# Delta output projection by Strassen products with tokens on partitions, weight sums moved to the heads

## The chip, the core and the metric

One NeuronCore of a Trainium2 chip runs the kernel. It has a matrix engine (PE, with its weight loads shown as PEld), a vector engine (DVE), a scalar engine (ACT), GpSimd (POOL) and a sync engine (SP) on whose queue this kernel puts all its transfers; 16 DMA engines carry them. The metric is the device time in microseconds (us) of one execution. Three timed runs of the kernel before gave 2934.2, 2929.16 and 2933.91: the median is 2933.91.

## What is computed

A hybrid decoder layer for 512 tokens and a model width of 2048, in float32: sliding-window attention and a gated DeltaNet run side by side on the same normalised input, their outputs are merged by gates and projected.

```python
h = rms_norm(x, norm_w) * (1.0 + scale) + shift
proj = h @ w_in                      # q, k, v, gate of attention; q, k, v, z, b, a of delta; merge gates
...
y_a = a_out @ w_o_swa                # 2048 -> 2048
...
o = gated_delta_rule(dq, dk, dv, g, beta)
o = rms_norm(o, dn_norm_w) * jax.nn.silu(dz)
y_b = o.reshape(B, T, DN_VAL).astype(x.dtype) @ w_o_dn      # 4096 -> 2048
y = jax.nn.sigmoid(mg_a) * y_a + jax.nn.sigmoid(mg_b) * y_b
return x + gate * (y @ w_out)        # 2048 -> 2048
```

The change is about `y_b`, the delta projection: 32 heads of 128 channels, 4096 in all, times a 4096 x 2048 matrix.

## The kernel before

**Products.** Each float32 factor is split into a high and a low part (`split`: ACT copies to the matrix type, DVE subtracts), and each product of 128x128 by 128x512 is three matmuls (`mm3`: lines 240, 241 and 242 in the kernel before): high x high, high x low, low x high. A *tile* is 128 output channels by 512 tokens (`channel_tile`): 16 steps of three matmuls, 48 in all, with the weights as the stationary factor and the tokens streaming, so that the result has channels on partitions.

**Weights.** `jobs` is a list of weight blocks of 1 MB in the order of use. `load_job` loads one into one of two `raw` buffers; `split_half` makes high and low parts of half a block (`whi`, `wlo`, 128x1024 each) in one of three buffers; `half_done` queues the next of both. The output stage takes three of five raw blocks from a further buffer (`rawo`).

**Order.** The program is written as generators. Every six matmuls `pump` takes a step of what is under way: `go` for work that belongs to the current tiles, `paced` for slow work at so many units per pump, `beside` for work at so many steps per pump. A scheduler then fixes each engine's own order; an engine does not go past an instruction that waits. `behind` ties an instruction to a place after the last matmul. All transfers stand in SP's order, and each of them also waits for the transfer that was issued eight places earlier.

**Stages.** Startup to about 180 us (conditioning, norm, first tiles); the keys; attention; the delta heads, 16 groups from about 1150 to 2187, of which each makes five tiles, loads two rows of decay masks (`E`, made on POOL and ACT), and writes two head outputs of 256 KB each to `o_d`; the delta projection (`branch_b`) from 2188.3 to 2595.2; the attention projection (16 tiles `os`) to 2769; the output projection by one step of Strassen's algorithm. For the last, `PRODUCTS` (line 34) lists seven products instead of eight: each with its name, the combination ("form") of the four quarters of the tokens' matrix that it takes, and either a quarter of the weights or one of four sums of quarters (`weight_sums`).

**The delta projection before.** `branch_b` works in two halves of 2048 channels. For each half it loads 16 blocks of `o_d`, splits them into `oh` and `ol`, computes two tiles of the merge gate (`ma` 12 and 13, then 14 and 15, by `merge_gate`), and then 16 tiles `od`. The first half is stored to `yb_d` with channels on partitions; the second adds it and multiplies with 1 + the merge gate from `mb_d`. Beside it run the output gate (`gate`: 16 loads of 1 MB, a sum on DVE, four matmuls) and `weight_sums` for the output projection (per set four loads of 512 KB, four additions of 128x1024 on DVE and four stores; eight sets).

## Time and profile before

| what | value |
|---|---|
| median of three timed runs | 2933.91 us |
| profiled execution | 2929.78 us, span 2928.0 us |
| instructions in the span | 38184 |
| DMA over the span | 498.34 MB, mean 170 GB/s |
| granted PE clock, mean | 0.995 |

Busy time by stage (us from the span's start; times in us, clock as a share of full speed):

| stage | length | PE | DVE | ACT | DMA share | GB/s |
|---|---|---|---|---|---|---|
| keys (180 to 600) | 420.0 | 420.0 | 277.4 | 197.1 | 0.53 | 166 |
| heads (1150 to 2187) | 1037.0 | 1029.4 | 554.7 | 403.5 | 0.38 | 119 |
| delta projection (2188.3 to 2595.2) | 406.9 | 399.8 | 213.6 | 112.5 | 0.84 | 293 |
| attention projection (2595.2 to 2769) | 173.8 | 173.8 | 88.0 | 53.7 | 0.59 | 192 |
| output projection (2769 to 2928) | 159.0 | 152.7 | 105.3 | 62.9 | 0.72 | 258 |

A stage in which PE's busy time equals its length is set by PE; where it falls short, PE waited for something. Matmuls overlap in the pipeline, so the cost of one is the distance between starts and not its duration. Idle time of an engine that nobody waits for costs nothing. The DMA share is the mean busy share of the 16 DMA engines.

### The profile page before, as it was taken

How to read it: one execution, taken by the hardware profiler on the slowest of the kernel's cores; microseconds unless marked ns; L12 is line 12 of the kernel's file. 1: busy time of each engine (PE TensorE's matmuls, PEld its weight loads, DVE VectorE, ACT ScalarE, POOL GpSimd, SP SyncE). 2: the span in 40 equal slices, each digit the busy share in tenths (PEclk: the TensorE clock that was granted, in tenths of full speed). 3: DMA queues.
4: the chain of work that ended last, by engine and by line, in shares of the span. 5: the costliest groups of instructions: out<-in, count | busy, mean ns of one | idle time of the engine just before them, and what ended most of it. 6: DMA issues, size and time to landing. Idle time of an engine off the chain costs nothing.

```text
span 2928.0 us, 38184 instructions
## 1 busy us (share of the span) xinstructions
PE 2861.4 (98%) x14524; PEld 2346.6 (80%) x14524; DVE 1755.9 (60%) x2903; ACT 1128.6 (39%) x2295; POOL 130.9 (4%) x124
## 2 busy tenths in 40 slices
PE   6899999999999999999999999999999999999999
PEld 5578888877877878888888888888887887888887
DVE  5756666868768666666544445455445555434666
ACT  3356443234444333333533334344333232222443
POOL 0001000100001010000000000001000000000000
PEclk8999999999999999999999999999999999999999
DMA  9856654322253243333533333343338988855794
GB/s 329 320 172 194 202 164 143 120 78 91 96 139 104 84 162 110 122 111 114 158 116 124 109 122 115 117 135 115 109 127 306 315 319 294 288 171 176 243 321 172
DMA packets 184874, 498.34 MB, mean 170 GB/s; under 512 B 75217, under 2 KB 77777, under 8 KB 147313
## 3 DMA queue, kind: packets, MB, share of 16 engines
q1 hardware_dynamic: 184690, 495.90, 51.1%
q8 instruction: 114, 1.87, 0.3%
q14 instruction: 70, 0.57, 0.1%
HBM read 415.26 MB, written 78.33 MB: 169 GB/s over the span
## 4 chain that ended last, share of the span: by engine, by line
PE 86%; DMA 5%; DVE 5%; ACT 2%; issue 1%; SPq 0%; POOL 0%; DVEq 0%; POOLq 0%; ACTq 0%
PE mm L240 23%; PE mm L242 23%; PE mm L241 23%; DMA oraw<-o_d 2%; PE m L241 2%; PE m L242 2%; PE m L240 2%; DMA gw<-in_w_ada_gate 1%; DVE wa L410 1%; PE pv L894 1%; PE po L913 1%; PE O L1259 1%; PE S L1208 1%; PE pP L281 1%; ACT sm L1232 1%
## 5 line engine op out<-in xcount | busy, mean ns | idle before, releaser
L240 PE MATMUL mm<-hh,whi 128*128 128x512 f32 x2784 | 1132.1, 407 | 2.8 <-ACT mth L270 2.8
L242 PE MATMUL mm<-hh,wlo 128*128 128x512 f32 x2784 | 1089.9, 391 | 1.1 <-DVE wlo L62 1.1
L241 PE MATMUL mm<-hl,whi 128*128 128x512 f32 x2784 | 1086.9, 390 | 0.0
L62 DVE TENSOR_TENSOR wlo<-raw,whi 128x1024 fp32r<-128x1024 f32 (+1 forms) x484 | 597.5, 1235 | 485.8 <-ACT whi L61 470.0
L61 ACT CAST whi<-raw 128x1024 fp32r<-128x1024 f32 (+1 forms) x484 | 504.7, 1044 | 914.7 <-PE mm L241 811.6
L242 PEld LDWEIGHTS mm<-hh,wlo 128*128 128x128 f32 x2784 | 522.8, 188 | 115.7 <-DVE wlo L62 1.6
L240 PEld LDWEIGHTS mm<-hh,whi 128*128 128x128 f32 x2784 | 523.9, 188 | 111.7 <-issue 8.3
L241 PEld LDWEIGHTS mm<-hl,whi 128*128 128x128 f32 x2784 | 524.5, 188 | 98.5 <-issue 0.5
L240 PE MATMUL mm<-oh,whi 128*128 128x512 f32 x512 | 201.7, 395 | 5.4 <-ACT oh L61 5.4
L241 PE MATMUL mm<-ol,whi 128*128 128x512 f32 x512 | 200.2, 391 | 0.5 <-DVE ol L62 0.5
L242 PE MATMUL mm<-oh,wlo 128*128 128x512 f32 x512 | 200.1, 391 | 0.1
L240 PEld LDWEIGHTS mm<-oh,whi 128*128 128x128 f32 x512 | 96.5, 188 | 27.7 <-ACT oh L61 7.1
L709 ACT ACTIVATE E<-E,neg_g 128x128 f32<-128x128 f32 x256 | 82.3, 394 | 86.0 <-POOL E L703 86.0
L241 PEld LDWEIGHTS mm<-ol,whi 128*128 128x128 f32 x512 | 96.6, 189 | 22.8 <-DVE ol L62 1.8
L242 PEld LDWEIGHTS mm<-oh,wlo 128*128 128x128 f32 x512 | 96.5, 188 | 20.6 <-DVE wlo L62 0.5
L738 DVE TENSOR_TENSOR atmp<-A 128x62 f32<-128x62 f32 (+30 forms) x124 | 109.4, 882 | 0.6
L746 DVE TENSOR_TENSOR A<-A,atmp 128x62 f32<-128x62 f32 (+30 forms) x124 | 107.9, 870 | 0.6
L841 POOL TENSOR_TENSOR qe<-qe,yq 128x512 f32<-128x512 f32 x32 | 52.8, 1669 | 955.8 <-DMA qe<-eg_rows 696.8
L887 DVE SCALAR_TENSOR_TENSOR r<-pp,neg_eg,vt 128x128 f32<-128x128 f32 x96 | 29.2, 346 | 86.3 <-PE pp L884 84.8
L1232 ACT ACTIVATE sm<-sm,mx,rs 128x256 f32<-128x256 f32 (+1 forms) x128 | 71.7, 562 | 3.5 <-DVE mx L1227 3.5
L573 DVE SCALAR_TENSOR_TENSOR yv<-mm,convh,yv 128x511 f32<-128x511 f32 (+2 forms) x96 | 71.3, 743 | 1.4
L703 POOL TENSOR_SCALAR_AFFINE_SELECT E<-E 128x512 f32<-128x512 f32 x64 | 48.2, 767 | 436.4 <-DMA E<-g_rows 366.1
(335 smaller groups left out, 2952.5 us busy)
## 6 DMA issues: line engine op xcount, KB each, us to landing
raw<-in_w_ch SPq DMA_DIRECT2D x158, 1024.0 KB
wa<-in_w_ada_ss SPq DMA_DIRECT2D x32, 1024.0 KB
raw<-in_w_od SPq DMA_DIRECT2D x32, 1024.0 KB
E<-g_rows SPq DMA_DIRECT2D x64, 256.0 KB
q<-in_w_out SPq DMA_DIRECT2D x32, 512.0 KB
gw<-in_w_ada_gate SPq DMA_DIRECT2D x16, 1024.0 KB
f_d<-q SPq DMA_DIRECT2D x32, 512.0 KB
raw<-in_w_os SPq DMA_DIRECT2D x16, 1024.0 KB
```

The lines of the kernel that those rows point to most:

```text
L61: self.nc.scalar.copy(out=hi, in_=src)
L62: self.nc.vector.tensor_tensor(out=lo, in0=src, in1=hi.bitcast(F32), op=ALU.subtract)
L240: nc.tensor.matmul(ps, lhsT=wh, rhs=xh, start=first, stop=False)
L241: nc.tensor.matmul(ps, lhsT=wh, rhs=xl, start=False, stop=False)
L242: self.last_mm = nc.tensor.matmul(ps, lhsT=wl, rhs=xh, start=False, stop=last)
L573: nc.vector.scalar_tensor_tensor(out=y[:, s:], in0=ps[:, : T - s], scalar=w[:, j : j + 1], in1=y[:, s:], op0=ALU.mult, op1=ALU.add)
L703: self.last_mask = self.nc.gpsimd.affine_select(out=E, in_=E, pattern=[[0, NTB], [1, P]], compare_op=ALU.is_ge, fill=NEG, base=0, channel_ ...
L709: self.nc.scalar.activation(E[:, c, :], E[:, c, :], AF.Exp, bias=self.neg_g[:, c, h : h + 1])
L738: eng.tensor_tensor(out=t, in0=A[:, m : m + 1, m + 1 :].to_broadcast([P, m, n]), in1=A[:, :m, m : m + 1].to_broadcast([P, m, n]), op=ALU.mult,
L746: self.behind(eng.tensor_tensor(out=A[:, :m, m + 1 :], in0=A[:, :m, m + 1 :], in1=t, op=ALU.add))
L841: self.behind(nc.gpsimd.tensor_tensor(out=qf, in0=qf, in1=q, op=ALU.mult), masks)
L1232: nc.scalar.activation(t, t, AF.Exp, scale=r[:, h : h + 1], bias=mx[:, h : h + 1], accum_out=den[:, h : h + 1])
```

## The change

The delta projection takes the form of the output projection. `w_od` is laid out in quarters ("quads"). Each half of channels h and each half n of the output columns is computed by the seven products of `PRODUCTS`, in the order m1, m7, m5, m2, m6, m4, m3: 28 products of 48 matmuls instead of 32 tiles of 48. The *tokens* are now the stationary factor and the weights stream, so results have tokens on partitions. `delta_forms` makes the seven forms of a half from `o_d`: for h = 0 five go to slots `f0` to `f4` and two through one staging buffer (`late`) to DRAM (`b_d`), to be loaded into `x0` and `x1` once the normalised input is no longer needed; for h = 1 two go to `x2` and `x3` and five through staging, to be loaded into `x`/`f` slots as these come free during (h, n) = (0, 1). `delta_evict` combines products into output blocks; h = 0 stores them to `yo_d`; h = 1 adds the stored ones, transposes each block on PE (16 groups of four) and multiplies with 1 + the merge gate. All four merge tiles now stand before the projection. Quarter sums of `w_od` (two sets of eight) join those of `w_out`, and all three run in the heads from group 4. The gate moves to the keys. One out of three weight blocks of the projection goes to a third raw buffer (`braw`).

```diff
-        for half in range(2):
-            ma(range(12 + 2 * half, 14 + 2 * half))
-            jobs += [(f"od{half}_{j}", a["w_od"][half, j]) for j in range(KT)]
+        ma(range(12, 16))
+        self.od0 = len(jobs)
+        for half in range(2):
+            for n in range(2):
+                for m, (_, _, q, f) in enumerate(PRODUCTS):
+                    for i in range(2):
+                        src = a["w_od"][half, 2 * q[0] + n, 2 * q[1] + i] if q else self.g_d[half, n, f, i]
+                        jobs.append((f"od{half}{n}_{m}_{i}", src))
+        self.od1 = len(jobs)
...
+            if self.od0 <= j < self.od1:
+                own = (j - self.od0) % 3 < 2
...
+            self.beside(self.gate(gt), 0.18, "gate")
...
+                if g == 4:
+                    sums = self.paced(self.weight_sums(ws), 1.55)
...
+            self.drain_slow(sums)
...
     def branch_b(self):
...
-            for half in range(2):
-                for kt in range(KT):
-                    raw = wk.tile([P, T], F32, tag="oraw", name="oraw")
-                    nc.sync.dma_start(out=raw, in_=self.o_d[half * KT + kt])
-                    self.split(oh[:, kt, :], ol[:, kt, :], raw)
-                for j in range(2):
-                    self.merge_gate("ma", 12 + 2 * half + j, self.ma_d)
...
+            self.go(self.delta_forms(wk, w, 0, A[0], 0), 1)
+            for j in range(12, 16):
+                self.merge_gate("ma", j, self.ma_d)
+            self.drain_live()
...
+            A[0].update(zip(forms[5:], more))
+            for f in forms[5:]:
+                self.form_load(0, f, A[0][f])
+            A[1].update(zip(forms, more[2:]))
+            build = self.paced(self.delta_forms(wk, w, 1, A[1], 1), 1.0)
...
+            for h, n, m in items:
+                name, form = PRODUCTS[m][:2]
+                if (h, n, m) == (0, 1, 1):
+                    self.drain_slow(build)
+                if h == 0 and n == 1 and 1 <= m <= 5:
+                    A[1][forms[m + 1]] = slots[m - 1]
+                    self.form_load(1, forms[m + 1], slots[m - 1])
...
+                ah, al = A[h][form]
+                for p in range(4):
+                    hi, lo = self.half(f"od{h}{n}_{m}_{p // 2}")
+                    for t in range(2):
+                        for k in range(2):
+                            kt, cols, tsl = 2 * p + k, slice(k * T, k * T + T), slice(t * P, (t + 1) * P)
+                            self.mm3(ps[name, t], (ah[:, kt, tsl], al[:, kt, tsl]), (hi[:, cols], lo[:, cols]), kt == 0, kt == 7)
...
+    def delta_forms(self, wk, w, h, direct, pause):
...
+        def put(kt, f, src):
+            if f in direct:
+                self.split(direct[f][0][:, kt, :], direct[f][1][:, kt, :], src)
+                return
+            k = staged.index(f) % 2
+            if k == 0:
+                late[0] = wk.tile([P, 2, 2, 256], F32R, tag="late", name="late", bufs=1)
+            t = late[0]
+            self.split(t[:, k, 0, :], t[:, k, 1, :], src)
+            for x in range(2):
+                nc.sync.dma_start(out=self.b_d[h, order[f], x][:, kt, :], in_=t[:, k, x, :].bitcast(F32))
...
+    def form_load(self, h, f, slot):
+        k = [p[1] for p in PRODUCTS].index(f)
+        for x in range(2):
+            self.nc.sync.dma_start(out=slot[x].bitcast(F32), in_=self.b_d[h, k, x])
...
+    def delta_evict(self, w, pf, h, n, name, ps, keep):
...
+            nc.sync.dma_start(out=prev, in_=self.yo_d[cc, t])
...
+            yield 2
+            TT(out=src, in0=src, in1=prev, op=ALU.add)
+            yield 1
+            pt = pf.tile([P, 4, P], F32, tag="tp", name="pty", bufs=2)
+            self.transpose4(pt.rearrange("p j t -> p (j t)"), lambda j: src[:, j * P : (j + 1) * P])
+            STT(out=th, in0=th, scalar=1.0, in1=pt, op0=ALU.add, op1=ALU.mult)
```

What stands where, on the engines that the change reorders. DVE before, after the last heads and at the first `od` tiles (`wlo` is the low part of a weight half, `ol` that of the heads' outputs, `gate_bc` the gate's sum):

```order
L62 TENSOR_TENSOR wlo_18601<-raw_18477,whi_18600 128x1024
L62 TENSOR_TENSOR ol_18387<-oraw_18412,oh_18386 128x512
L62 TENSOR_TENSOR ol_18387<-oraw_18416,oh_18386 128x512
L62 TENSOR_TENSOR wlo_18633<-raw_18541,whi_18632 128x1024
L62 TENSOR_TENSOR ol_18387<-oraw_18420,oh_18386 128x512
L62 TENSOR_TENSOR ol_18387<-oraw_18424,oh_18386 128x512
L1435 SCALAR_TENSOR_TENSOR gate_bc_18501<-gw_18581,silu_c_118,gate_bc_18501 128x2048
L62 TENSOR_TENSOR ol_18387<-oraw_18428,oh_18386 128x512
L62 TENSOR_TENSOR ol_18387<-oraw_18432,oh_18386 128x512
L62 TENSOR_TENSOR wlo_18667<-raw_18541,whi_18666 128x1024
```

DVE in the changed kernel at merge tile 14, whose two halves are `wlo_19178` and `wlo_19209` (`f0l` to `f4l` are forms, `o0` and `o1` the heads' outputs, `late` the staging buffer):

```order
L62 TENSOR_TENSOR wlo_19178<-raw_18875,whi_19177 128x1024
L62 TENSOR_TENSOR f0l_18838<-o0_18865,f0h_18837 128x256
L62 TENSOR_TENSOR f1l_18840<-s3_18877,f1h_18839 128x256
L1074 TENSOR_TENSOR o0_18865<-o0_18865,o1_18866 128x256
L62 TENSOR_TENSOR f3l_18844<-o1_18866,f3h_18843 128x256
...
L62 TENSOR_TENSOR f4l_18846<-o0_19075,f4h_18845 128x256
L1074 TENSOR_TENSOR o0_19109<-o0_19109,o1_19110 128x256
L62 TENSOR_TENSOR wlo_19209<-raw_18875,whi_19208 128x1024
```

Between two weight halves stood two to five operations; between these two stand 76 of 128x256, counting those that the list merges.

SP in the changed kernel, second column half of h = 0: `raw_20466` is the last weight block of product m4, `raw_20506` the first of m3, the last product of (0, 1); `f0h` to `f3l` are forms of h = 1 that come back:

```order
L213 DMA raw_20466<-g_d_65 128x2048
L1061 DMA b_d_18829<-late_20207 128x256 x4
L1136 DMA yo_d_18830<-c11_20468 128x512
L1096 DMA f0h_18837<-b_d_18829 128x2048
L1061 DMA b_d_18829<-late_20217 128x256 x4
L1096 DMA f0l_18838<-b_d_18829 128x2048
L1061 DMA b_d_18829<-late_20227 128x256 x2
L1096 DMA f1h_18839<-b_d_18829 128x2048
...
L1096 DMA f3l_18844<-b_d_18829 128x2048
L1136 DMA yo_d_18830<-c11_20480 128x512
L213 DMA raw_20506<-in_w_od 128x2048
```

Between these two weight blocks eight form loads of 1 MB now stand (the row of "..." has four of them); before, weight blocks of this stage had between them loads and stores of 256 or 512 KB and at most one of 1 MB.

SP in group 9 of the heads before, and in the changed kernel (`qe` and `E` are rows of decays, `o_d` the head outputs, `q..` a quarter of weights for the sums, `g_d` where a sum goes):

```order
L200 DMA raw_14421<-in_w_ch 128x2048
L820 DMA qe_14449<-eg_rows_1267 128x512
L820 DMA qe_14455<-eg_rows_1267 128x512
L698 DMA E_14895<-g_rows_1266 128x512
L698 DMA E_14897<-g_rows_1266 128x512
```

```order
L213 DMA raw_14655<-in_w_ch 128x2048
L844 DMA qe_14683<-eg_rows_1275 128x512
L844 DMA qe_14689<-eg_rows_1275 128x512
L1172 DMA q00_14710<-in_w_od 128x1024
L1177 DMA g_d_65<-q01_14375 128x1024
L1172 DMA q11_14714<-in_w_od 128x1024
L722 DMA E_15157<-g_rows_1274 128x512
L1172 DMA q01_14716<-in_w_od 128x1024
L978 DMA o_d_1126<-zh_14299 128x512
L978 DMA o_d_1126<-zh_14408 128x512
L213 DMA raw_14794<-in_w_ch 128x2048
L722 DMA E_15159<-g_rows_1274 128x512
```

The two mask loads stood together; now three transfers of the sums stand ahead of the first, and a sum load, two stores of head outputs and a weight block ahead of the second.

More of the change, by code (lines that the diff above doesn't have):

```diff
@@ L196, in load_job @@
             src = self.jobs[j][1]
-            own = j < self.out0 or (j - self.out0) % 5 < 2
+            if j == self.od1 and not self.paused:
+                self.paused = True
+                return
+            if self.od0 <= j < self.od1:
+                own = (j - self.od0) % 3 < 2
+            else:
+                own = j < self.out0 or (j - self.out0) % 5 < 2
             pool, tag = (self.wraw, "raw") if own else (self.oraw, "rawo")
@@ L630, in delta_heads @@
                 self.step_slow(self.solves)
+            ws = sb.enter_context(tc.tile_pool(name="wsum", bufs=1, reuse_waits="tile"))
+            sums = None
             for g in range(KH):
+                if g == 4:
+                    sums = self.paced(self.weight_sums(ws), 1.55)
                 if g == 8:
@@ L990, in branch_b @@
-            self.drain("gate")
-            self.drain_slow(sums)
+            self.pmm = pf = es.enter_context(tc.tile_pool(name="pmmb", bufs=4, space=PSUM, reuse_waits="tile"))
+            fm = es.enter_context(tc.tile_pool(name="bf", bufs=1, side="right", reuse_waits="tile"))
+            slots = [tuple(fm.tile([P, 8, 256], F32, name=f"f{i}{x}").bitcast(F32R) for x in "hl") for i in range(5)]
+            fm.tile([P, 8], F32, name="alignb")
+            wk = es.enter_context(tc.tile_pool(name="bwk", bufs=1, side="right", reuse_waits="tile"))
@@ new lines, in branch_b @@
+            fx = hx.enter_context(tc.tile_pool(name="bx", bufs=1, reuse_waits="tile"))
+            more = [tuple(fx.tile([P, 8, 256], F32, name=f"x{i}{x}").bitcast(F32R) for x in "hl") for i in range(4)]
+            A[0].update(zip(forms[5:], more))
[3 more added lines that the diff above has]
+            build = self.paced(self.delta_forms(wk, w, 1, A[1], 1), 1.0)
+            ps, keep = {}, {}
+            items = [(h, n, m) for h in range(2) for n in range(2) for m in range(7)]
```

183 lines of the change are left out of this document (136 added, 47 removed).

## The prediction

> **What bounds the kernel now.** I read the page first (busy time, chain, groups), then windows over the delta projection, then the waits in it, then single timelines.
>
> ```profile
> PE 2861.4 (98%) x14524; PEld 2346.6 (80%) x14524; DVE 1755.9 (60%) x2903; ACT 1128.6 (39%) x2295; POOL 130.9 (4%) x124
> ...
> PE 86%; DMA 5%; DVE 5%; ACT 2%; issue 1%; SPq 0%; POOL 0%; DVEq 0%; POOLq 0%; ACTq 0%
> ...
> L240 PE MATMUL mm<-oh,whi 128*128 128x512 f32 x512 | 201.7, 395 | 5.4 <-ACT oh L61 5.4
> L241 PE MATMUL mm<-ol,whi 128*128 128x512 f32 x512 | 200.2, 391 | 0.5 <-DVE ol L62 0.5
> L242 PE MATMUL mm<-oh,wlo 128*128 128x512 f32 x512 | 200.1, 391 | 0.1
> ```
>
> PE is busy for 98% of the span and holds 86% of the chain that ended last, so a matmul less is time less, as long as nothing that feeds PE comes late instead. The delta projection is three groups of 512: 1536 matmuls. Their means overlap (they are pipelined), so their price is a rate:
>
> ```profile
> 2188.30:2210.20 21.90, 21.89 (x96) 18.13 (x97) 15.03 (x17) 8.44 (x13) 0.00 (x0) 1.00 0.89 314
> 2210.20:2387.50 177.30, 175.41 (x770) 143.77 (x769) 96.21 (x73) 47.52 (x58) 0.00 (x0) 1.00 0.90 314
> 2387.50:2410.60 23.10, 21.97 (x97) 17.89 (x96) 11.21 (x12) 9.64 (x14) 0.00 (x0) 1.00 0.87 302
> 2410.60:2595.20 184.60, 180.50 (x778) 146.70 (x778) 91.13 (x102) 46.85 (x57) 0.00 (x0) 0.99 0.78 269
> 2600.00:2700.00 100.00, 100.00 (x443) 82.84 (x442) 45.55 (x69) 28.41 (x40) 0.00 (x0) 1.00 0.52 169
> ```
>
> After each stretch stand its length, busy time of PE, PEld, DVE, ACT and POOL with counts, granted clock, DMA share and GB/s. An undisturbed stretch (the last row) has 443 matmuls in 100 us: **0.2257 us** each, 10.83 for a tile of 48. The first four rows are this part of the program: two merge tiles, half 0, two merge tiles, half 1, 406.9 us for 36 tiles, where 36 x 10.83 = 390. So some 17 us go to other things, and the DMA share is already 0.78 to 0.90.
>
> ```profile
> PE mm L240 <- ACT oh L61: 5.4, 4, 2.1
> PE mm L240 <- ACT mth L270: 1.4, 1, 1.4
> PE mm L242 <- DVE wlo L62: 1.1, 1, 1.1
> PE mm L241 <- DVE ol L62: 0.5, 2, 0.2
> ```
>
> PE's waits there sum to 8.4 us (waiter, who was waited for, total, times, longest). What comes after one of them, in PE's timeline (start, duration, then the instruction):
>
> ```profile
> 2424.77 0.49 PE L240 MATMUL mm<-oh,whi 128*128 128x512 f32 x1 [2.07 <-ACT oh L61]
> ...
> 2426.91 0.63 PE L240 MATMUL mm<-oh,whi 128*128 128x512 f32 x1
> 2427.33 0.63 PE L241 MATMUL mm<-ol,whi 128*128 128x512 f32 x1
> ...
> 2429.47 0.63 PE L240 MATMUL mm<-oh,whi 128*128 128x512 f32 x1
> 2429.89 0.45 PE L241 MATMUL mm<-ol,whi 128*128 128x512 f32 x1
> ```
>
> Seven steps from 2426.91 to 2429.89 are 0.426 apart instead of 0.226: a stretch at half rate, with what lies at its edges about **1.6 us**, after waiting. I use that for each new long wait.
>
> **The change, part by part.** (h,n) is a half of the channels and a half of the output columns; each is seven products of 48 matmuls.
>
> Removed: 1536 - 28 x 48 = 192 matmuls of the same shape, 192 x 0.2257 = **43.3 us**. The split of the heads' outputs no longer stands between tiles of a running projection, so I count the 8.4 us of waits and the 1.6 us of slow clock as gone: 53.3 in all. The rest of the 17 us holds the four gate matmuls, which only move.
>
> Added, transposes:
>
> ```profile
> 2178.74 0.39 PE L242 MATMUL mm<-hh,wlo 128*128 128x512 f32 x1
> 2178.97 0.60 PE L281 MATMUL pto<-ident,osb 128*128 128x128 f32 x4
> 2179.33 0.48 PE L240 MATMUL mm<-hh,whi 128*128 128x512 f32 x1
> 2179.64 0.40 PE L241 MATMUL mm<-hl,whi 128*128 128x512 f32 x1
> ```
>
> From 2178.74 to 2179.64 lie two matmuls and four transposes: 0.90 - 2 x 0.2257 = 0.44 us a group. Sixteen groups: **7.1 us**, on PE, nothing hides them.
>
> Added, token forms of half 0, made before the first product:
>
> ```profile
> 2727.26 1.22 DVE L62 TENSOR_TENSOR wlo<-raw,whi 128x1024 fp32r<-128x1024 f32 x1
> 2728.40 0.42 DVE L62 TENSOR_TENSOR a12l<-m,a12h 128x256 fp32r<-128x256 f32 x1
> 2728.74 0.41 DVE L1301 TENSOR_TENSOR yq<-yq,m 128x256 f32<-128x256 f32 x1
> 2729.07 0.42 DVE L62 TENSOR_TENSOR late<-m,late 128x256 fp32r<-128x256 f32 x1
> 2729.41 0.41 DVE L1303 SCALAR_TENSOR_TENSOR yq<-yq 128x256 f32<-128x256 f32 x1
> ...
> L61 ACT CAST whi<-raw 128x1024 fp32r<-128x1024 f32 (+1 forms) x484 | 504.7, 1044 | 914.7 <-PE mm L241 811.6
> ```
>
> The first five are DVE's timeline in the output stage, the last a group of the page. DVE's 128x256 operations start 0.337 us apart; a weight half takes it 1.14 and ACT 1.04. In the new order 76 such operations stand on DVE between the two weight halves of merge tile 14, where before two to five stood between halves. The casts they follow stand on ACT behind the eviction of tile 12, so they begin when tile 12 ends. Call that T0. DVE reaches the second half at T0 + 1.04 + 1.14 + 76 x 0.337 and is done 1.14 later: T0 + 28.9. PE has tile 13 and the first half of tile 14 to do, 16.3 us. Lower end of the **stall: 12.7 us**. The upper end comes from the staging buffer, of which there is one: each of about seven rounds stores it in four pieces.
>
> ```profile
> 1398.48 2.01 ACT L751 COPY atmp<-A 64x1024 f32<-64x1024 f32 x1 [0.81 <-DVE A L746]
> ...
> 1403.45 2.03 ACT L751 COPY atmp<-A 64x1024 f32<-64x1024 f32 x1 [1.07 <-DMA ta_d<-atmp]
> ...
> 1400.52 0.49 SPq L752 DMA_DIRECT2D ta_d<-atmp  x1
> ```
>
> A store frees its buffer 2.9 us after issue (1400.52 to 1403.45), and an issue takes SP 0.49: a round lasts 4 x 0.49 + 2.9 = 4.9 us, seven 34, so T0 + 34 and a stall of 18. I take 15.5, the middle, plus one stretch at half rate: **17.1** (range 13 to 20).
>
> Added, the traffic of (0,1). Summing the sizes of the transfers that SP issues from its first weight to its last gives 34.9 MB: 14.7 of weights (14 loads of 1 MB; a half now has 28 where it had 16), 10.5 of forms of half 1 loaded back, 6.0 of forms stored, 1.6 of the delta heads' outputs, 2.1 of results. What the DMA engines have shown when nothing else limited them:
>
> ```profile
> 2480.00:2500.00 20.00, 20.00 (x90) 16.55 (x89) 11.19 (x14) 5.79 (x7) 0.00 (x0) 1.00 0.99 346
> 30.00:70.00 40.00, 24.83 (x168) 18.50 (x169) 22.15 (x30) 10.16 (x16) 0.00 (x0) 0.74 1.01 423
> ```
>
> The second is startup (1 MB loads), the first has smaller stores and loads among large ones; both show DMA engines with nothing left (shares 0.99 and 1.01). Seven products take PE 75.8 us; the bytes take 82.4 at 423 and 100.9 at 346: **stall 6.6 to 25**. The order says where: eight form loads of 1 MB stand on SP in one run ahead of the first weights of (0,1)'s last product. They need 8.4 MB / 423 = 20 us, while PE holds only the work of four raw loads, 4 x 5.42 = 21.7, less 2.3 for splitting. A chain of staging rounds (4.9 us each, more behind a 1 MB load) beside weights of 5.42 us each could bring it to 35. The mixture of large loads and small stores lies between the rows: 385 GB/s, 90.6 us, 15, plus one stretch at half rate: **16.6**.
>
> The Trainium skill ("DMA: Bandwidth & Descriptors", Specifications) gives a limit of about 358 GB/s from HBM for one core. Startup's 423 GB/s is above it, so the trace disagrees. By the page's figure the 34.9 MB would, as an estimate, take 97 us, and the sum would be some 7 us higher.
>
> Added, (0,0) and half 1: (0,0) issues 27.8 MB in 75.8 us, which fits at 423 and overruns by 4.5 at 346: I take **3**, range 0 to 8 as two staged forms come back just after the stall. Half 1 issues about 41.4 MB in 151.7 us, 273 GB/s, as half 1 did before (269), so its weights are covered. But each of 16 transposes waits for an add that waits for a load two steps earlier. The nearest row is the adds of the weight sums (count, busy us, mean ns, idle before):
>
> ```profile
> L1018 DVE TENSOR_TENSOR q<-q,q 128x1024 f32<-128x1024 f32 x32 | 39.1, 1223 | 22.4 <-DMA q<-in_w_out 22.1
> ```
>
> They waited 22.4 / 32 = 0.7 us each; sixteen give 0 to 11, I take **5**, since two steps of pumping hide most.
>
> Moved and tripled, the weight sums in the heads. First the heads' windows before the change, then PE's only waits in the first of them:
>
> ```profile
> 1150.00:1390.00 240.00, 232.51 (x1235) 192.35 (x1235) 162.42 (x274) 90.64 (x217) 23.04 (x16) 0.99 0.37 118
> 1390.00:2160.00 770.00, 770.00 (x4061) 641.17 (x4061) 381.80 (x724) 305.06 (x700) 45.68 (x42) 1.00 0.38 120
> ```
>
> ```profile
> PE ptv L281 <- DVE yv L580: 7.5, 4, 2.5
> ```
>
> 96 adds x 1.223 = 117 us of DVE, 100.7 MB of loads and stores over about 790 us (group 4 begins near 1400), 127 GB/s on top of 120. From 1390 to 2160 PE never waits, with DVE at 382 of 770 us, DMA share 0.38. After, DVE is near 499 of 770, 65%, and DMA near 0.8. The nearest row with such a DVE is 1150 to 1390: 162 of 240, 68%, and there PE waited 7.5 us for yv. At that pace 770 us hold 24. There is also a matter of queue: in the new order sum loads and result stores stand on SP ahead of, and in three groups between, a group's two loads of decay masks (E), and a sum load can wait there for a store just issued; behind it wait POOL, ACT, DVE and at last ptv on PE. Ends 0 (all inside the slack that the quiet stretch shows) and 24; I take **12**, the middle: DVE's load is the second row's, but the solves that ran beside it then are over.
>
> The gate moves from this part to the keys: four matmuls as before, 16 loads at a slow pace beside a PE that the projection's tiles keep filled. I cost it at 0; without that cover it is at most the rest of the 17 us, 17 - 10 = 7, paid there instead of here. The 32 first-set adds leave the projection; DVE was no limit there.
>
> Sum: 7.1 + 17.1 + 16.6 + 3 + 5 + 12 = 60.8 against 53.3: **+7.5 us**. The profiled execution took 2929.78 (span 2928.0), 4.1 below the median of 2933.91, and the three runs spread over 5.0; 2929.78 + 7.5 = 2937.3, and I add half of that 4.1: **2939**.
>
> **Rivals.** The output stage before the change:
>
> ```profile
> 2700.00:2900.00 200.00, 200.00 (x884) 165.68 (x883) 124.02 (x168) 80.81 (x103) 0.00 (x0) 1.00 0.77 270
> ```
>
> *The DMA engines keep up* (not slower): one mechanism, the rate in (0,1) and the heads. At 423 GB/s the stall is 6.6 + 1.6, (0,0), half 1 and the heads are hidden: 7.1 + 17.1 + 8.2 = 32.4, net -20.9: 2909. It decides when the traffic terms (36.6 in my sum) stay below 23; for it speaks that the output projection, built alike, two forms of seven staged too,, runs without PE waits, against it the 34.9 MB and the run of eight loads.
>
> *Heads hide the sums*: all else as forecast, the 12 gone: net -4.5, 2925, no measurable change. For it: no PE wait at all in 770 us; against it, DVE at 65%.
>
> *DMA falls to the slower row*: 346 GB/s, 25 + 1.6 in (0,1), 4.5 in (0,0), 11 in half 1, 24 in the heads, stall at tile 14 of 20: 93 against 53.3, +40: 2970; with staging rounds deciding (35) 2980. Against it: large rows prevail.
>
> **Numbers.** Forecast 0.36, DMA keeps up 0.35, sums hidden 0.17, DMA slow 0.12. A measurement of this kernel tells about 0.2%, 5.9 us, from no change. Faster 0.35, same 0.17, slower 0.48. The range runs from just under the first rival to past the last: 2905 to 2985; the forecast alone has 2936 to 2955.
>
> **What would show it.** Right: 1344 matmuls with token forms as weights; PE idle 13 to 18 us once at tile 14 with wlo as releaser; a second wait of 7 to 25 us for wlo, behind a raw load, near the end of (0,1), with DMA at 0.95 or more; sixteen steps of 0.44 us for transposes; PE waits for ptv or pv between 1400 and 2190. Wrong: no wait at tile 14 (DVE did the forms earlier), DMA above 423 GB/s in (0,1), no waits in the heads, or waits above 11 us in half 1 or 7 in the keys.

## The result: 1.5% slower

The changed kernel takes 2975.09 us in the median of four runs (2973.74 to 2979.18) against 2933.18 of the kernel before: ratio **1.0148, 95% interval 1.0130 to 1.0165**, some 42 us more. The forecast was 2939, the range 2905 to 2985: right in direction, and 36 us short. The profiled execution has a span of 2977.4 us against 2928.0: 49.4 more, which the following accounts for. (It is the slowest of the four, and the one of the kernel before lies near the fast end; hence 49 and not 42.)

The page after (engines' busy time, then the chain that ended last):

```profile
PE 2846.9 (96%) x14396; PEld 2327.0 (78%) x14396; DVE 1959.4 (66%) x3215; ACT 1195.8 (40%) x2423; POOL 138.3 (5%) x124
...
PE 36%; DMA 6%; DVE 2%; ACT 1%; issue 1%; SPq 1%; POOL 0%; DVEq 0%; ACTq 0%; POOLq 0%
```

PE has 128 instructions less (192 matmuls gone, 64 transposes come), yet its busy time fell by 14.5 us only, where 43.3 - 7.1 = 36.2 were to be expected. Part of the missing 21.7 us is matmuls at half rate, as the two timelines below show them after long waits: steps of 0.42 to 0.44 us between matmuls of 512 columns number 108 from 180 us on, against 64 before, some 9 us. The rest is not traced. The chain's shares add up to less than half here, so I read the waits and windows instead. PE's waits from the last heads to the end of the delta projection (total, times, longest), then stretches of the span (heads, merge tiles, the 14 products of half 0, those of half 1; PE busy, PEld, DVE, ACT, POOL, clock, DMA share, GB/s):

```profile
PE m L255 <- ACT whi L61: 27.1, 4, 22.1
PE mm L255 <- ACT whi L61: 15.1, 1, 15.1
PE pty L296 <- DVE m L1144: 11.7, 5, 8.0
PE m L256 <- DVE wlo L62: 6.0, 6, 2.1
PE mm L255 <- ACT mth L285: 1.4, 1, 1.4
PE mm L257 <- DVE wlo L62: 1.0, 1, 1.0
PE pty L296 <- DVE c L1144: 0.5, 1, 0.5
```

```profile
1166.90:2202.20 1035.30, 1019.62 (x5350) 846.20 (x5349) 655.89 (x1092) 397.81 (x918) 71.16 (x58) 0.99 0.63 207
2209.00:2271.90 62.90, 46.40 (x192) 37.47 (x193) 43.15 (x99) 28.55 (x67) 0.00 (x0) 0.86 0.87 289
2271.90:2467.80 195.90, 162.72 (x674) 128.96 (x674) 113.69 (x171) 80.58 (x121) 0.00 (x0) 0.92 0.88 317
2467.80:2643.40 175.60, 163.42 (x738) 133.45 (x737) 116.31 (x135) 72.77 (x81) 0.00 (x0) 0.97 0.79 263
```

These are bounded by instructions of the program (the first and last transposes of heads' outputs, the first matmuls with `f0h` and `x2h`, the last transposes of results), so that they can be set beside the steps of the prediction. Half 0 is (0,0) and (0,1), half 1 is (1,0) and (1,1). The merge tiles and products take 62.9 + 195.9 + 175.6 = 434.4 us; the whole part took 406.9 before: **+27.5**. The heads take 1035.3 against 1020.8 (1160.3 to 2181.1) before: **+14.5**. They begin 6.6 later: the gate's four matmuls stand ahead of them now, and the keys have 3.2 us of waits that they had not before. Together 48.6 of the 49.4.

What stands at the two places that the prediction named. The first, at merge tile 14 (PE's timeline):

```profile
2236.96 0.39 PE L256 MATMUL mm<-hl,whi 128*128 128x512 f32 x1
2252.44 0.79 PE L255 MATMUL mm<-hh,whi 128*128 128x512 f32 x1 [15.09 <-ACT whi L61]
2253.03 0.63 PE L256 MATMUL mm<-hl,whi 128*128 128x512 f32 x1
2254.67 0.80 PE L257 MATMUL mm<-hh,wlo 128*128 128x512 f32 x1 [1.02 <-DVE wlo L62]
```

PE went on at 2254.67 when DVE had finished the second half of tile 14 (T0, the end of tile 12, was at about 2220.3: T0 + 34). DVE came to the first half of tile 14 late already, having waited 3.5 us for a load of `o_d`; ACT waited 0.4 us in all for the staging buffer from 2209 to 2256. The 15.1 us are written down to a `whi` because the scheduler had put two matmuls of tile 15 ahead of that one, and these waited for tile 15's weights, whose load stood on SP behind staging stores. A row names the last releaser, not everything that was late.

The second, near the end of (0,1): SP's timeline, then PE's:

```profile
2428.67 0.80 SPq L1061 DMA_DIRECT2D b_d<-late  x2
2429.56 0.43 SPq L1096 DMA_DIRECT2D f1h<-b_d  x1
...
2433.83 0.47 SPq L213 DMA_DIRECT2D raw<-in_w_od  x1
```

```profile
2431.27 0.39 PE L257 MATMUL m<-whi,x0l 128*128 128x512 f32 x1
2453.71 1.22 PE L255 MATMUL m<-whi,x1h 128*128 128x512 f32 x2 [22.05 <-ACT whi L61]
...
2455.56 0.63 PE L257 MATMUL m<-whi,x1l 128*128 128x512 f32 x1
2455.99 0.63 PE L255 MATMUL m<-whi,x1h 128*128 128x512 f32 x1
...
2459.40 0.57 PE L255 MATMUL m<-whi,x1h 128*128 128x512 f32 x1
```

The weights of the last product are issued at 2433.83, behind six reloads of 1 MB issued from 2429.56 on, when PE had already run dry. After the wait PE starts matmuls 0.43 us apart until 2459.4. The DMA engines had room before this wait and none in it (half 0's products up to the wait, then the wait):

```profile
2271.90:2431.70 159.80, 148.67 (x625) 118.06 (x624) 105.59 (x164) 74.47 (x115) 0.00 (x0) 0.98 0.85 297
2431.70:2453.70 22.00, 0.00 (x0) 0.00 (x0) 0.70 (x2) 1.09 (x2) 0.00 (x0) 0.60 1.01 409
```

### The profile page after: what moved, and what is told of

It is laid out like the page before. It is cut to its first block, busy times and chain, and to the rows that moved or that the text cites. A ratio compares the mean times of both kernels' runs of the same rounds, so it can differ in the third digit from the quotient of the medians.

```text
span 2977.4 us, 39003 instructions
## 1 busy us (share of the span) xinstructions
PE 2846.9 (96%) x14396; PEld 2327.0 (78%) x14396; DVE 1959.4 (66%) x3215; ACT 1195.8 (40%) x2423; POOL 138.3 (5%) x124
## 5 line engine op out<-in xcount | busy, mean ns | idle before, releaser
L255 PE MATMUL mm<-hh,whi 128*128 128x512 f32 x2784 | 1137.3, 409 | 17.9 <-ACT whi L61 15.1
L62 DVE TENSOR_TENSOR wlo<-raw,whi 128x1024 fp32r<-128x1024 f32 (+1 forms) x532 | 657.8, 1238 | 509.7 <-ACT whi L61 496.6
L61 ACT CAST whi<-raw 128x1024 fp32r<-128x1024 f32 (+1 forms) x532 | 553.9, 1044 | 974.5 <-PE mm L256 690.8
L255 PEld LDWEIGHTS mm<-hh,whi 128*128 128x128 f32 x2784 | 525.8, 189 | 128.8 <-ACT whi L61 15.5
L1176 DVE TENSOR_TENSOR q<-q,q 128x1024 f32<-128x1024 f32 x96 | 120.0, 1250 | 5.8 <-DMA q<-in_w_out 5.6
L727 POOL TENSOR_SCALAR_AFFINE_SELECT E<-E 128x512 f32<-128x512 f32 x64 | 55.7, 884 | 458.0 <-DMA E<-g_rows 369.7
L426 DVE SCALAR_TENSOR_TENSOR wa<-wa,silu_cb 128x2048 f32<-128x2048 f32 x24 | 54.8, 2283 | 6.8 <-DMA silu_cb<-silu_d 6.8
L938 ACT COPY osb<-po 128x256 f32<-128x256 f32 x64 | 23.9, 373 | 86.2 <-PE po L937 85.2
L814 ACT COPY vt<-ptv 128x512 f32<-128x512 f32 x32 | 18.7, 583 | 83.3 <-PE ptv L296 83.3
L920 ACT COPY vn<-pv 128x256 f32<-128x256 f32 x64 | 23.7, 370 | 63.6 <-PE pv L918 63.6
L937 PE MATMUL po<-vn,E 128*128 128x128 f32 x256 | 46.8, 275 | 0.0
```

The costliest lines, as they stand in the source:

```text
L61: self.nc.scalar.copy(out=hi, in_=src)
L62: self.nc.vector.tensor_tensor(out=lo, in0=src, in1=hi.bitcast(F32), op=ALU.subtract)
L255: nc.tensor.matmul(ps, lhsT=wh, rhs=xh, start=first, stop=False)
L937: nc.tensor.matmul(po[:, e, :], lhsT=M[e][:, c, :], rhs=vn[:, e, :], start=c == 0, stop=True)
L1176: self.behind(nc.vector.tensor_tensor(out=q[f], in0=q[x], in1=q[y], op=ALU.add))
```

## Experiments

Times are given as ratios to the kernel before on the same chip, since chips differ (its median was 2927.64 to 2933.18 in these calls). The changed kernel stands at 1.0148.

### Late reloads

```diff
-                if h == 0 and n == 1 and 1 <= m <= 5:
-                    A[1][forms[m + 1]] = slots[m - 1]
-                    self.form_load(1, forms[m + 1], slots[m - 1])
+                k = {10: 2, 12: 3, 14: 4, 16: 5, 18: 6}.get(7 * (2 * h + n) + m)
+                if k:
+                    A[1][forms[k]] = slots[k - 2]
+                    self.form_load(1, forms[k], slots[k - 2])
```

> Only the five reloads of forms of half 1 are moved: they stand at products 10, 12, 14, 16 and 18 of 28 instead of 8 to 12, so that no run of eight stands on SP ahead of the weights of product 13. Theory (queue): the 22.1 us wait at 2431 comes from loads that nobody needs yet standing ahead of an urgent weight block; it falls to 0 to 5 us, its 3 us of half clock goes too, and the time falls by 18 to 25 us against the changed kernel, to about 2950 to 2957. Rival (bytes): the DMA engines were at their limit for the whole of (0,1); the same bytes then make a wait of 10 us or more elsewhere in (0,1) or (1,0) and the time falls by less than 10.

Ratio 1.0121 (1.0106 to 1.0136), 2963.27 us. The 22 us wait became one of 6.2, but in all only some 0.3% went: half 0's products took 184.3 us instead of 195.9, now with 55.8 MB instead of 62.1, since some reloads moved to half 1. That is the gain of less than 10 us that the rival named, though the DMA engines were not at their limit (share 0.86): the queue was the place of the wait, and not the whole of its cause.

### Spread forms

```diff
             put(kt, "a12", r1[:, lo])
-            if pause:
-                yield 2.0
+            yield 2.0 if pause else 1
...
             put(kt, "a22", r1[:, hi])
-            if pause:
-                yield 2.0
+            yield 2.0 if pause else 1
```

> Only the forms of half 0 are spread: two pauses of one pump are added per block, so that they are made over three merge tiles instead of one. Between the two weight halves of merge tile 14 stand 27 operations on DVE instead of 76. Theory (order on DVE and ACT): the 15.1 us wait for whi and the 1.0 us for wlo go, with 2.6 us of half clock: the time falls by 14 to 19 us, to 2956 to 2961. Rival (the one staging buffer and its stores are the pace): the wait is paid at the last merge tiles or at the first product instead, and the time falls by less than 6.

Ratio 1.0149 (1.0133 to 1.0166), 2970.86 us: no gain. PE's waits in the part:

```profile
PE m L255 <- ACT whi L61: 37.1, 6, 24.2
PE pty L296 <- DVE m L1142: 11.3, 5, 6.9
PE m L256 <- DVE wlo L62: 4.5, 6, 2.4
PE mm L257 <- DVE wlo L62: 1.2, 1, 1.2
```

The wait at the merge tiles is gone (`mm` has 1.2 us left), so the order on DVE had been what held tile 14 up. But the products' own waits (`m`) rose from 27.1 to 37.1, and half 0's products took 210.3 us instead of 195.9. PE came earlier to work whose data came no earlier. The rival's sign came true; which of buffer, queue or bytes set that pace was open.

### Without the sums of the delta weights

```diff
-                        src = a["w_od"][half, 2 * q[0] + n, 2 * q[1] + i] if q else self.g_d[half, n, f, i]
+                        src = a["w_od"][half, 2 * q[0] + n, 2 * q[1] + i] if q else a["w_od"][half, 2 * (f // 2) + n, 2 * (f % 2) + i]
...
-        sets = [(a["w_od"][0], self.g_d[0]), (a["w_od"][1], self.g_d[1]), (a["w_out"], self.f_d)]
+        sets = [(a["w_out"], self.f_d)]
```

> The sums of quarters of the delta weights are left out (64 of 96 additions, 67 of 101 MB in the heads); the products that took them take plain quarters instead, with the same bytes and matmuls. Theory: the heads' 14.5 us of added time (from 1160 to 2202) come from the sums; the sums of the output weights end in the first third of it, so 8 to 12 us of the 14.5 go, and the total falls by as much, to 2963 to 2967. Rival: the added time in the heads has another cause (the gate's move, the clock): the total changes by less than 3.

This kernel leaves the sums out, so that its output is not the layer's; only its time is of use. Ratio 1.0105 (1.0089 to 1.0122), 2959.24 us: 0.43% or 12 us less than the changed kernel, as expected in size, not in place. The heads took 1025.9 us, where late reloads on the same chip took 1030.3: 4.4 us for two thirds of the sums. Most of the rest went at the merge tiles, where one wait of 9.9 us stood in place of the 16. There the last set of sums is drained in the changed kernel, and its loads and stores stand on SP ahead of the loads of `o_d`. So the sums cost at both ends.

### Sums on GpSimd

```diff
-                            self.behind(nc.vector.tensor_tensor(out=q[f], in0=q[x], in1=q[y], op=ALU.add))
+                            self.behind(nc.gpsimd.tensor_tensor(out=q[f], in0=q[x], in1=q[y], op=ALU.add))
```

> The 96 additions of the weight sums are put on GpSimd instead of DVE; their loads and stores stay. If the heads wait because DVE is loaded with 117 us more, the waits of ptv on yv after 1400 (6.9 us) go and the time falls by 6 to 12 us. If they wait because decay masks come late behind the sums' transfers, nothing is gained; and since the masks are made on GpSimd, additions of about 3 us each ahead of them would add 0 to 20 us.

Ratio 1.0248 (1.0226 to 1.0270), 3002.07 us: some 29 us more than the changed kernel, beyond the 0 to 20 expected. The heads took 1067.2 us (1162.8 to 2230.0). PE's largest waits there:

```profile
PE ptv L296 <- DVE yv L596: 20.2, 6, 6.0
PE pd L933 <- DVE vs L925: 17.8, 11, 3.7
```

Taking the additions off DVE did not take the waits away but made them longer: the additions take GpSimd 2.4 us each in the median, and the masks that this chain needs are made there too. So GpSimd is no place for them. Whether DVE's load or the masks' place on SP makes the heads' waits stays open: the run, as expected for that case, delays the masks itself.

### Both reorderings, then two buffers, then another queue

Late reloads and spread forms together:

> Late reloads and spread forms together. In each of the two alone the one wait went but short waits for whi at the starts of products grew: 16 us gone at merge tile 14 gave 2.4 us in the whole stage. Theory now: in (0,0) and (0,1) weight blocks stand on SP behind stores of the one staging buffer, which wait for casts, which wait for the store before; this chain is the pace, so removing waits elsewhere only moves them. Then both together gain no more than late reloads alone, 6 to 14 us against the changed kernel, with waits for whi of 12 us or more in (0,0) and (0,1). If the two edits were independent, about 25 us would go and the ratio to before would be about 1.006.

Ratio 1.0119 (1.0099 to 1.0140): together they give what late reloads give alone, as spread forms alone had given nothing. The waits that each removes do not add up to time. Then with two staging buffers:

```diff
-                late[0] = wk.tile([P, 2, 2, 256], F32R, tag="late", name="late", bufs=1)
+                late[0] = wk.tile([P, 2, 2, 256], F32R, tag="late", name="late", bufs=2)
...
-            w = lambda name: wk.tile([P, T], F32, tag="w", name=name, bufs=10)
+            w = lambda name: wk.tile([P, T], F32, tag="w", name=name, bufs=8)
```

> As both together, with two staging buffers instead of one (and 8 working tiles instead of 10 to make room). If the single buffer's round (casts, issue, store, 4.9 us) is the pace, the waits for whi and wlo in (0,0) and (0,1) fall to under 6 us and the time falls by another 10 to 20 us, to a ratio of 0.998 to 1.004. If the bytes are the pace, nothing changes by more than 3 us.

Ratio 1.0119 (1.0100 to 1.0138): no change in the time. Half 0's products fell from 197.9 to 182.9 us (59.3 MB at 324 GB/s, DMA share 0.93), but 6.9 more were lost between the heads and them and the waits of the last transposes grew from 13.3 to 23.1, with two working tiles less, which may be the reason (no run separates the two). So half 0's products gained 15 us, and the run paid that back elsewhere. Then the staging stores on GpSimd's queue, with one buffer:

```diff
-                nc.sync.dma_start(out=self.b_d[h, order[f], x][:, kt, :], in_=t[:, k, x, :].bitcast(F32))
+                nc.gpsimd.dma_start(out=self.b_d[h, order[f], x][:, kt, :], in_=t[:, k, x, :].bitcast(F32))
```

> As both together, with the stores of the staging buffer issued on GpSimd's queue instead of SP's, so that no weight load stands behind a store that waits for a cast; one buffer. If SP's order is what delays the weights, the waits for whi fall to under 6 us, as with two buffers or better, even though a round is no shorter. If the buffer's round delays the casts of weights on ACT and DVE themselves, waits for wlo and whi stay above 10 us. If the bytes are the pace, no change.

Ratio 1.0176 (1.0157 to 1.0195): worse. In that run ACT's casts into the buffer come at these times in the merge tiles, each after a wait for the store before:

```profile
2231.32 0.72 ACT L61 CAST late<-o 128x256 fp32r<-128x256 f32 x2 [4.51 <-DMA b_d<-late]
...
2236.57 0.71 ACT L61 CAST late<-o 128x256 fp32r<-128x256 f32 x2 [0.66 <-DMA b_d<-late]
...
2246.51 0.71 ACT L61 CAST late<-o 128x256 fp32r<-128x256 f32 x2 [5.29 <-DMA b_d<-late]
```

A round took 5 to 10 us there, and weight halves on DVE came 14.9 and 4.8 us late for PE: the merge tiles took 25 us more than with both reorderings alone. The buffer's round does hold up the engines when it is slow enough.

### All of these, with early loads for the last product

```diff
+                pre = {}
+                if h == 1 and name == "m3":
+                    for t in range(2):
+                        pre[t] = self.prev_load(w, 2 + n, t)
```

`prev_load` issues the two loads of `delta_evict` (stored block and merge gate); the eviction then takes them from `pre`.

> Late reloads, spread forms, two staging buffers, staging stores on GpSimd's queue, and the loads for the last product of each column half of half 1 (stored block and merge gate) issued before that product's matmuls. The last edit takes the 8 us wait of the last transposes on the add of the stored block: to under 2 us, worth 7 to 9 with its half clock. All together: ratio to before 0.985 to 0.998 if the waits were all queue and buffer; above 1.004 if bytes.

Ratio 1.0163 (1.0140 to 1.0186). The last transposes waited longer (12.8, 7.8 and 4.1 us), probably because with eight working tiles the early loads take the tiles that the evictions need. A miss as a whole; but half 0's products took 171.0 us instead of 195.9, with 57.2 MB at 335 GB/s, so that stage gained some 25 us from these edits together, and merge tiles and half 1 lost it again (some 9 and 18 us).

### Unsplit staging

All variants so far had half 0 move 55 to 66 MB in 171 to 210 us. The next halves the staging bytes: a form is stored as one float32 and split after it returns.

```diff
-            self.split(t[:, k, 0, :], t[:, k, 1, :], src)
-            for x in range(2):
-                nc.sync.dma_start(out=self.b_d[h, order[f], x][:, kt, :], in_=t[:, k, x, :].bitcast(F32))
+            nc.sync.dma_start(out=self.b_d[h, order[f]][:, kt, :], in_=src)
...
-        for x in range(2):
-            self.nc.sync.dma_start(out=slot[x].bitcast(F32), in_=self.b_d[h, k, x])
+        raw = slot[1].bitcast(F32)
+        self.nc.sync.dma_start(out=raw, in_=self.b_d[h, k])
+
+        def halves():
+            for p in range(4):
+                sl = slice(2 * p, 2 * p + 2)
+                self.split(slot[0][:, sl, :], slot[1][:, sl, :], raw[:, sl, :])
+                yield 1
+
+        self.go(halves(), 10)
```

The form s4 gets a tile of its own, so that no store reads a tile that is overwritten next; there are 11 working tiles.

> Forms that go through DRAM are stored unsplit (one float32 instead of high and low part), straight from the working tiles, without the staging buffer, and are split after they come back, four pieces a form. The order of loads stays as in the changed kernel. In all variants so far half 0's 14 products took what their bytes need at 290 to 335 GB/s (62.1 MB in 195.9 us, 55.8 in 184.3, 59.3 in 182.9), whatever order, buffer or queue. Theory (bytes at this mixture's rate): some 12 MB go, 50 MB at 317 GB/s are 158 us, near PE's 151.7: half 0's products fall to 155 to 170 us, the total by 25 to 38 us, ratio to before 1.002 to 1.006. Rival (order on SP: the run of reloads ahead of product 13's weights): the wait of 22 us only halves, the total falls by 8 to 15.

Ratio **1.0015 (1.0006 to 1.0025)**, 2933.17 us: 38 us of the 42 are gone, with the program's order as it was. Half 0's products:

```profile
2262.50:2417.80 155.30, 154.26 (x673) 125.95 (x672) 116.24 (x157) 82.65 (x109) 0.00 (x0) 1.00 0.89 316
```

155.3 us where PE needs 151.7, with the clock at 1.00. But this variant takes away three things at once: bytes, the staging buffer with its casts, and the run of reloads, which now stand one by one between weights. (It also has one working tile more.) What SP waited for in (2271.9, 2417) shows the difference, first in the changed kernel, then here:

```profile
SPq L1061 <- ACT late L61: 65.9, 20, 8.0
SPq L1061 <- DVE late L62: 14.7, 16, 1.6
```

```profile
SPq L213 <- DVE wlo L62: 48.8, 20, 5.8
```

In the changed kernel SP stands 81 us of 145 at stores whose cast is not done, with weight loads behind. Here it stands at weight loads whose buffer is still in use, which means that it is as far ahead as the buffers allow. Why the casts were late shows in what ACT waited for in the changed kernel, over the same stretch:

```profile
ACT whi L61 <- DMA raw<-g_d: 30.1, 12, 5.3
ACT whi L61 <- DMA raw<-in_w_od: 20.3, 7, 5.4
ACT whi L61 <- PE m L257: 9.5, 9, 1.8
ACT late L61 <- DMA b_d<-late: 5.5, 5, 1.7
```

The buffer itself held ACT up for 5.5 us only. ACT waited 50 us for weight loads, with casts into the buffer standing behind; SP waited for these casts, with weight loads standing behind. The two orders hold each other up, and a second buffer leaves that as it is: with two, SP still stood 60 us of 143 at such stores.

### The bytes alone

Unsplit staging with every piece stored twice and every form loaded twice:

```diff
             nc.sync.dma_start(out=self.b_d[h, order[f]][:, kt, :], in_=src)
+            nc.sync.dma_start(out=self.b2_d[h, order[f]][:, kt, :], in_=src)
...
+        self.nc.sync.dma_start(out=slot[0].bitcast(F32), in_=self.b2_d[h, k])
         self.nc.sync.dma_start(out=raw, in_=self.b_d[h, k])
```

> As unsplit staging, but every piece is also stored to a second place in DRAM and every form is also loaded from there (into the slot that the split then overwrites), so that the staging bytes are those of the changed kernel again, about 62 MB in half 0's products, without its staging buffer, with no cast ahead of a store, and with the reloads one by one between weight loads. Theory (bytes): half 0's products take 62 MB at 300 to 335 GB/s, 185 to 200 us, ratio to before 1.011 to 1.018. Rival (the chain cast, store, next cast through one buffer, on which SP waits): the bytes cost little, half 0's products stay at 155 to 170 us, ratio 1.001 to 1.006.

Ratio 1.0084 (1.0069 to 1.0100), 2953.83 us: between the two theories. Half 0's products (window and transfers):

```profile
2264.10:2441.90 177.80, 160.56 (x673) 126.67 (x672) 116.14 (x159) 82.34 (x109) 0.00 (x0) 0.96 0.94 347
```

```profile
DMA packets 21679, 61.65 MB, mean 347 GB/s; under 512 B 2415, under 2 KB 12655, under 8 KB 16367
```

Nearly the same bytes as in the changed kernel (61.65 MB for 62.13) take 177.8 us instead of 195.9, at a DMA share of 0.94 instead of 0.88. So of the 40.6 us between the changed kernel and unsplit staging in half 0, **22.5 are the bytes** (177.8 - 155.3, the issues on SP of the second copy included) and **18.1 the way they were staged**. By the ratios it is 0.69% and 0.64%. The second part is buffer, casts and reload order together, and no run separates them; late reloads alone gave 0.27%.

### Unsplit staging with the reorderings

Late reloads, spread forms, and the result stores of half 1 on GpSimd's queue (nothing is waiting for them until the next stage):

```diff
-            nc.sync.dma_start(out=self.yb_d[4 * cc : 4 * cc + 4, :, tsl].rearrange("j p t -> p j t"), in_=th)
+            nc.gpsimd.dma_start(out=self.yb_d[4 * cc : 4 * cc + 4, :, tsl].rearrange("j p t -> p j t"), in_=th)
```

> Unsplit staging with spread forms, late reloads, and the result stores of half 1 on GpSimd's queue, so that no load stands on SP behind a store that waits for DVE. With the bytes out of the way the two reorderings should now be worth what they remove: merge tile 14's 13 to 16 us go, and the last transposes' wait of 8 us falls to under 4. Ratio to before 0.993 to 1.000. If the bytes were not the limit, it stays above 1.006.

Ratio **0.9963 (0.9950 to 0.9976)**, 2918.64 us: faster than both kernels, by 0.5% against unsplit staging alone. That is not the reorderings' gain alone: of the 13 us that the part lost, 7 went in half 1 (178.9 to 172.0), where the result stores were moved. The merge tiles gave 15.5, and half 0's products took 9.4 of them back (155.3 to 164.7 us), so that the wait was moved in part here too. PE's waits in the part:

```profile
PE pty L296 <- DVE m L1144: 8.6, 4, 6.9
PE m L256 <- DVE wlo L62: 4.7, 6, 1.5
PE m L255 <- ACT whi L61: 2.5, 2, 1.9
PE mm L255 <- ACT mth L285: 1.4, 1, 1.4
PE pty L296 <- DVE c L1144: 0.7, 1, 0.7
```

Of the 49 us of waits for weights (27.1 + 15.1 + 6.0 + 1.0) 7 are left. The last transposes' wait fell from 8.0 to 6.9 only, where under 4 was expected. In the last, the reload of the attention's output (for the next stage) is paced faster:

```diff
-            yield 1.2
+            yield 0.9
```

> As unsplit staging with all reorderings, with the reload of the attention input paced at 0.9 instead of 1.2 pumps a step, so that it ends before the last product, whose block loads stood on SP behind one such load for 6 us. The last transposes' wait of 6.9 us should fall to under 3 and the time by 3 to 6 us against it, to a ratio of 0.994 to 0.996; if the wait is the latency of the two loads alone, no change.

Ratio 0.9962 (0.9949 to 0.9975), 2918.25 us. The longest wait of the last transposes fell from 6.9 to 3.6, the total of PE's waits in the part from 17.9 to 16.3, and the time not measurably: no gain from it, where 3 to 6 us were expected.

## Why the prediction was right in sign and short in size

Term by term, in the profiled executions: the delta projection was to take 4.5 us less (7.1 + 17.1 + 16.6 + 3 + 5 - 53.3) and took 27.5 more; the heads were to take 12 more and took 14.5; nothing was to be added ahead of them, and they began 6.6 later. That the total still lies in the range is due to the range's width of 80 us.

**Removed matmuls, transposes: right.** 128 instructions less; where a group of transposes did not wait (2519.75) it cost 0.46 us, 0.44 were predicted.

**Stall at merge tile 14: right, its upper end by luck.** Predicted 12.7 to 18 us of waiting, 15.5 taken; measured 15.1 + 1.0, with the end at the upper bound, T0 + 34. That bound was made of the staging buffer's rounds, and these cost ACT 0.4 us there. What came on top of the order on DVE (T0 + 28.9) was mostly loads of `o_d` that stood on SP behind the last sums and behind staging stores: without the sums of the delta weights the wait was 9.9. Spread forms show that the order on DVE was its cause, and also that it was worth nothing by itself as long as the next 14 products were short of data.

**(0,1) and (0,0): mechanism right, size wrong.** This is the step that failed. It took 385 GB/s "between the rows" and 16.6 + 3 us. Half 0's products took 195.9 us, 44.2 above PE's 151.7. The bytes were as counted (27.8 + 34.9 MB predicted, 62.1 measured); the rate was 317 GB/s, below both rows that I had set as its ends. Those rows showed DMA engines with nothing left, 423 GB/s for large loads and 346 for a mixture; the same bytes without the staging buffer reached that second row (347). What pulled it below was that the DMA engines were *not* always given work: their share was 0.85 before the 22 us wait and 1.01 in it, as the prediction's sign had asked for (0.95 or more). While they had room, SP stood 81 us at stores that waited for casts. I had such a chain in the text (rounds of 4.9 us beside weights of 5.42) but as an upper end, not as something that adds to the bytes, and as rounds of the buffer, where ACT's waits show weight loads and casts that hold each other up. That this chain makes the whole of the 18.1 us beyond the bytes is not shown, since the order of the reloads went with it.

**Half rate after waits: mis-sized.** I counted two stretches of 1.6 us. PE's waits grew by 64.5 us, and its busy time was 21.7 us above what the count of instructions gives; some 9 us of that are the 44 more steps at half rate. After the 22 us wait alone it was thirteen steps or so of 0.43 instead of 0.226, 2.7 us, and waits of 2.0 and 2.2 us (2340.4, 2391.0) were followed by six and four such steps.

**Half 1: too low.** 5 predicted, with more than 11 named as a sign of being wrong; it came, with waits of 12.2, of which 8.0 at the last block, whose loads stood on SP behind result stores, one of which waited 4.4 us for DVE (2628.18 to 2633.29). Nothing follows in the stage that could cover it.

**Heads: right in size, 12 for 14.5.** In the ten other runs that leave the heads alone they took 1030.3 to 1034.7 us, 9.5 to 13.9 above before. The reason is open: I had put the number on DVE's load, and the run that took it off DVE put a delay on GpSimd instead. Two thirds of the sums were worth 4.4 us there. What the sums cost at the merge tiles, through their drained last set, I had not seen.

**The gate: put at nothing.** The heads began 6.6 us later, with 3.2 of new waits in the keys and the gate's four matmuls, which had left the delta projection. The prediction's own limit for it was 7.

**The rivals.** The size came out near the third rival, DMA falling to the slower row (2970), by other shares: half 0's products lost 44 us where it had 31, the heads 14.5 where it had 24. The first rival, DMA engines that keep up, needed 423 GB/s, which half 0's products as a whole did not reach in any run (289 to 347). What the Trainium skill says of 358 GB/s for one core ("DMA: Bandwidth & Descriptors", Specifications) was nearer to what the mixture gave than startup's 423 was: 347 GB/s at a share of 0.94. But startup exceeded it, and so did the same stretch of that run once its staging stores were over:

```profile
2384.00:2428.00 44.00, 32.47 (x131) 25.25 (x132) 30.52 (x39) 22.07 (x30) 0.00 (x0) 0.88 1.01 422
```

Before it, from 2264.1 to 2384, the same run moved 321 GB/s at a share of 0.92. So it is the mixture, and not the limit that the Trainium skill states, that made the 347. Whether small packets do it (12655 of 21679 under 2 KB) stays open: in the run with all reorderings the stores went by GpSimd's queue, 2318 of 13344 packets were under 2 KB, and 335 GB/s took a share of 0.93.

## What to carry to other kernels

An algorithm with fewer multiplications was paid for in bytes and in order: count the transfers of each stretch against the time that the matmuls there take, and take as rate what a mixture of that kind has shown, less the time in which the queue waits for casts. Where several edits each remove a wait and none gains time, something common sets the pace; change the amount (here the bytes of the staged forms, by storing them before the split) before the order. And look for a store that waits for a late result on the queue from which weights are prefetched: here it held that queue for 81 us of 145. Another queue alone was no cure (1.0176); storing what needs no cast was.

## What the hardware showed

- Matmul steps doubled (0.43 for 0.226 us) after long waits, for some 6 us: 2252.44 to 2258.3 after 15.1 us, 2453.7 to 2459.4 after 22 us. Waits of 2.03 and 2.16 us (2340.4, 2391.0) were followed by six and four, a wait of 2.08 us (2386.2) by none.
- With more than half of the packets under 2 KB, DMA engines that were busy 94% of the time moved 347 GB/s; within that stretch it was 422 GB/s at a share of 1.01 while nearly all was loads of 1 MB, and at startup 423 with such loads.
- 128x1024 additions in float32 took 1.25 us on DVE and 2.4 us in the median on GpSimd (up to 5.8).
